# Two plain units instead of four ahead of the paired products, in three of four feed-forward half steps

## The chip, the cores and the metric

The kernel runs on one core of a Trainium2 chip. The metric is the device time of one execution in microseconds (us), as the median of several runs. TensorE (PE) multiplies matrices from SBUF, the on-chip memory, into PSUM, its accumulators of eight banks. VectorE (DVE), ScalarE (ACT) and GpSimd (POOL) do the elementwise work, and SyncE (SP) starts most transfers from the main memory. Each engine works through its own list of instructions in a fixed order, and waits where an input is not there yet.

## What is computed

A two-layer encoder over 512 tokens of width 1024, all in 32-bit floats. Each layer is a feed-forward half step, a token mixer, a cross-attention and another feed-forward half step, so there are four half steps in all. Only they are touched by the change:

```python
def swiglu(h, w_in, w_out):
    a, b = jnp.split(h @ w_in, 2, axis=-1)
    return (jax.nn.silu(a) * b) @ w_out

for l in range(2):
    x = x + 0.5 * swiglu(rms_norm(x, ffn1_norm[l]), ffn1_w_in[l], ffn1_w_out[l])
    ...  # token mixer, cross-attention
    x = x + 0.5 * swiglu(rms_norm(x, ffn2_norm[l]), ffn2_w_in[l], ffn2_w_out[l])
```

The hidden width is 2816, or 22 hidden tiles of 128.

## The kernel before

**Three multiplications for one.** A float matrix product is made of three on fp32r operands (`mm3`, L472 to L475): each operand is split into a rounded high half and a low half that is the rest, and the products high by high, high by low and low by high are added up in PSUM. So every operand, weights too, costs one ScalarE cast (the high half, `whi` for weights, L444) and one VectorE subtraction (the low half, `wlo`, L445); for activations both stand in `split_to` (L602 and L603).

**A half step** has three kinds of work, in the order that `ffn_order` writes out by hand.

- A *plain unit* (`pair_unit`) makes the two halves a and b of one hidden tile: 8 input blocks by 2 columns by 3, so 48 multiplications with 512 columns. `gated` then makes silu(a)·b: VectorE multiplies by the norm's row (L652), ScalarE applies silu (L653), GpSimd multiplies (L654), VectorE multiplies by b (L655), and the result is split (L602, L603).
- A *pair* makes two hidden tiles by Strassen's scheme in Winograd's form. Its seven products (`S1`, `A11`, `A12`, `S2`, `S3`, `A22`, `S4`) have 24 multiplications each, with 256 columns. Each product takes a block of weights that is split when it is due, and a moving operand `mv`, made once per half step by the task `combos`. That task first normalizes the whole input into the buffers `xn` (L674). Four of the moving operands are sums of quarters of the input (`total`, L684, and its split); three are quarters that are written in place over `xh` and `xl` (`in_place`), which the plain units must have finished reading. The weights of S1, S2 and S4 are sums as well: the transfers add two blocks, and VectorE adds A11 (L452) and later A12 (L456) in the same buffer. Each pair also has seven VectorE additions that combine the products (L754), two multiplications (L778) and two splits.
- An *output tile* (`out_tile`) multiplies the hidden tiles of one block with `w_out`, three multiplications of 512 columns for each hidden tile, and VectorE adds the result to x (L728). Eight such tiles belong to each block of hidden tiles.

Before the change every half step has 4 plain units, then 2 output tiles of their block, and then 9 pairs in blocks of 3, 2, 2 and 2, with two or four output tiles within each pair; 8 output tiles end it.

**What sets the order.** The program order is as the source emits it. Weights are split three parts ahead of their use (`LOOK` in `take`), into four buffers, so a split waits for the matrix engine to be done with the part four before it. Tasks such as `combos` advance by one step at each `tick`, after a gated unit or an output tile. A scheduler then lays each engine's list out, and may draw an instruction ahead of one that it expects to wait; that list is what runs.

## Time and profile before

| What | Before |
|---|---|
| Median of three runs | 2607.92 us (2606.85 to 2607.95) |
| The profiled execution, device time | 2608.38 us |
| Its span, first instruction to last | 2606.5 us |
| TensorE busy | 2571.5 us, 99% of the span |
| VectorE busy | 1826.2 us, 70% |
| ScalarE busy | 1321.3 us, 51% |
| GpSimd busy | 337.2 us, 13% |
| Mean granted clock of TensorE | 0.996 of full speed |

The profile's page gives the busy time of each engine and the chain of waits that ended last. The timeline lists instructions with start, duration and the idle time in front of them, in brackets with what ended it. For pipelined engines a duration is longer than the distance to the next start; where instructions follow without a wait, this text goes by that distance. The half steps begin at about 0, 958, 1305 and 2243 us of the span; mixer and cross-attention lie between the first and the second, and between the third and the fourth.

### The profile page before, as it was taken

Reading aid. Unit: us, or ns where it says so; the run is one execution under the profiler, and the core shown is the slowest. Engines: PE = TensorE matmul, PEld = TensorE weight load, DVE = VectorE, ACT = ScalarE, POOL = GpSimd, SP = SyncE. Lnnn points to the kernel's source line nnn. Section 1 sums busy time; section 2 is a strip of 40 time slices with the busy share of each in tenths; the row PEclk is TensorE's granted clock in tenths of the full one; section 3 lists DMA queues with packets and bytes.
Section 4 is the critical chain, followed back from the end, with each engine's and each line's share of the span. In section 5 each row is a group of like instructions: output and inputs, shape, how many; then the busy total and the mean of one; then the engine's idle time right before and its main releaser. Section 6 shows DMA issues by size and latency. Waiting matters only on the chain.

```text
span 2606.5 us, 36643 instructions
## 1 busy us (share of the span) xinstructions
PE 2571.5 (99%) x14784; PEld 2260.2 (87%) x14784; DVE 1826.2 (70%) x2536; ACT 1321.3 (51%) x1861; POOL 337.2 (13%) x294
## 2 busy tenths in 40 slices
PE   8999999999999999999999999999999999999997
PEld 7999978878888888999889999887888888899996
DVE  7867786776655558767788677877675664787675
ACT  5433457876634444434454333579575353444344
POOL 1000035100121021000110000351000300200001
PEclk9999999999999999999999999999999999999999
DMA  6555442222233253645517553321223234345541
GB/s 204 155 153 145 114 137 73 73 82 81 89 112 115 83 176 97 171 137 146 161 65 194 146 146 85 131 95 57 81 81 97 97 130 126 117 135 157 144 124 65
DMA packets 78234, 311.36 MB, mean 119 GB/s; under 512 B 8304, under 2 KB 14064, under 8 KB 69104
## 3 DMA queue, kind: packets, MB, share of 16 engines
q1 hardware_dynamic: 66976, 269.18, 31.0%
q0 software_dynamic: 10368, 37.75, 8.7%
q8 instruction: 115, 1.88, 0.3%
q10 hardware_dynamic: 720, 2.09, 0.2%
q14 instruction: 55, 0.45, 0.1%
HBM read 306.90 MB, written 2.10 MB: 119 GB/s over the span
## 4 chain that ended last, share of the span: by engine, by line
PE 90%; ACT 5%; DVE 3%; DMA 1%; POOL 1%; issue 1%; DVEq 0%; ACTq 0%; SPq 0%; POOLq 0%
PE ps L474 29%; PE ps L473 29%; PE ps L475 29%; PE ps L1132 1%; PE ps L1120 1%; PE ps L1103 1%; ACT whi L444 1%; DVE wlo L445 1%; DVE slot L603 0%; DMA x<-in_xt 0%; DVE xl L537 0%; POOL slot L654 0%; ACT L909 0%; ACT L919 0%; PE ps L1433 0%
## 5 line engine op out<-in xcount | busy, mean ns | idle before, releaser
L473 PE MATMUL ps<-slot,whi 128*128 128x256 f32 (+1 forms) x2436 | 812.9, 335 | 6.9 <-ACT slot L602 6.9
L474 PE MATMUL ps<-slot,whi 128*128 128x256 f32 (+1 forms) x2436 | 814.3, 334 | 0.9 <-DVE slot L603 0.9
L475 PE MATMUL ps<-slot,wlo 128*128 128x256 f32 (+1 forms) x2436 | 810.9, 334 | 0.0
L444 ACT CAST whi<-stage 128x1024 fp32r<-128x1024 f32 (+3 forms) x394 | 346.4, 881 | 509.5 <-PE ps L474 412.9
L473 PE MATMUL ps<-xh,whi 128*128 128x512 f32 (+1 forms) x1760 | 597.6, 340 | 6.6 <-ACT xh L536 3.3
L474 PE MATMUL ps<-xl,whi 128*128 128x512 f32 (+1 forms) x1760 | 594.5, 338 | 0.3 <-DVE xl L537 0.3
L475 PE MATMUL ps<-xh,wlo 128*128 128x512 f32 (+1 forms) x1760 | 594.2, 338 | 0.0
L445 DVE TENSOR_TENSOR wlo<-stage,whi 128x1024 fp32r<-128x1024 f32 (+3 forms) x394 | 415.5, 1056 | 148.0 <-ACT whi L444 145.3
L473 PEld LDWEIGHTS ps<-slot,whi 128*128 128x128 f32 x2436 | 463.1, 190 | 54.0 <-ACT slot L602 10.0
L474 PEld LDWEIGHTS ps<-slot,whi 128*128 128x128 f32 x2436 | 463.7, 190 | 46.0 <-DVE slot L603 2.4
L475 PEld LDWEIGHTS ps<-slot,wlo 128*128 128x128 f32 x2436 | 463.1, 190 | 46.2
L444 ACT CAST whi<-slot 128x1024 fp32r<-128x1024 f32 x252 | 265.3, 1053 | 433.4 <-PE ps L474 318.5
L473 PEld LDWEIGHTS ps<-xh,whi 128*128 128x128 f32 x1760 | 334.3, 190 | 45.9 <-DVE slot L1256 4.9
L474 PEld LDWEIGHTS ps<-xl,whi 128*128 128x128 f32 x1760 | 334.4, 190 | 38.3 <-DVE xl L537 1.6
L475 PEld LDWEIGHTS ps<-xh,wlo 128*128 128x128 f32 x1760 | 334.2, 190 | 35.1
L445 DVE TENSOR_TENSOR wlo<-slot,whi 128x1024 fp32r<-128x1024 f32 x252 | 307.8, 1222 | 66.0 <-ACT whi L444 66.0
L754 DVE TENSOR_TENSOR slot<-ps,slot 128x512 f32<-128x512 f32 x252 | 170.6, 689 | 140.9 <-PE ps L475 139.7
L428 POOL DMA_DIRECT2D slot<-in_wts x72 | 62.9, 874 | 1204.3 <-DMA slot<-in_wts 1053.3
L602 ACT CAST slot<-slot 128x512 fp32r<-128x512 f32 (+2 forms) x165 | 106.0, 649 | 147.3 <-POOL slot L1290 44.6
L728 DVE SCALAR_TENSOR_TENSOR x<-ps,x 128x512 f32<-128x512 f32 (+1 forms) x161 | 110.5, 686 | 88.7 <-PE ps L475 88.6
L603 DVE TENSOR_TENSOR slot<-slot,slot 128x512 fp32r<-128x512 f32 (+2 forms) x165 | 123.0, 754 | 51.7 <-ACT slot L602 51.7
L603 DVE TENSOR_TENSOR slot<-ps,slot 128x512 fp32r<-128x512 f32 (+1 forms) x144 | 92.8, 655 | 38.7 <-ACT slot L602 38.1
(205 smaller groups left out, 2667.7 us busy)
## 6 DMA issues: line engine op xcount, KB each, us to landing
slot<-in_wts SPq DMA_DIRECT2D x180, 512.0 KB, 4.2
stage<-in_wts SPq DMA_DIRECT2D x141, 512.0 KB, 3.6
stage<-in_wts SPq DMA_DIRECT2D x68, 1024.0 KB, 4.8
slot<-in_wts POOLq DMA_DIRECT2D x72, 512.0 KB, 6.1
stage<-in_wts SPq DMA_DIRECT2D x24, 768.0 KB, 6.0
slot<-in_memt SPq DMA_DIRECT2D x6, 512.0 KB, 3.7
slot<-in_bd SPq DMA_DIRECT2D x4, 512.0 KB, 3.6
out<-slot SPq DMA_DIRECT2D x8, 256.0 KB, 2.3
```

The costliest lines, as they stand in the source:

```text
L428: pool.dma_start(out=t, in_=a22 if nm == "S1" else a11, accum_op=ALU.add)
L444: mark["whi"] = act.copy(hi[:, 0:n], t).ins
L445: dve.tensor_tensor(lo[:, 0:n], t, hi[:, 0:n].bitcast(F32), op=ALU.subtract)
L473: pe.matmul(ps, lhsT=ah, rhs=bh, start=start, stop=False)
L474: pe.matmul(ps, lhsT=ah, rhs=bl, start=False, stop=False)
L475: pe.matmul(ps, lhsT=al, rhs=bh, start=False, stop=stop)
L602: act.copy(hi, src)
L603: return dve.tensor_tensor(lo, src, hi.bitcast(F32), op=ALU.subtract).ins
L728: dve.scalar_tensor_tensor(x[:, m, cs], ps, 0.5, x[:, m, cs], op0=ALU.mult, op1=ALU.add)
L754: dve.tensor_tensor(r.f, ps, other.f, op=op)
L1103: pe.matmul(ps, lhsT=qt[e].r[:, c0:c0 + P], rhs=kk.r[:, k0:k0 + 512], start=part == 0, stop=part == 1)
L1120: pe.transpose(ps[:, kt * P:(kt + 1) * P], pexp.f[:, i * 512 + kt * P:i * 512 + (kt + 1) * P], ident)
```

## The change

The first half step keeps its 4 units and its blocks. The other three get 2 units, blocks of 3, 2, 3 and 2 pairs, and all 8 output tiles of the units' block (now of two hidden tiles) ahead of the first pair; the first three pairs then have no output tiles within them, and the later ones have 4, 4, 3, 3, 2, 4 and 4. So two hidden tiles of each of these half steps are made by a pair and no longer by two units. In all four half steps the products on quarters in place, A11 and A12, come ahead of S1, and `combos` makes the two in-place operands before the sums. The weights of a block of two hidden tiles are split for two output tiles at a time (`per_part`).

```diff
-NPLAIN = 4
-PAIR_BLOCKS = (3, 2, 2, 2)
-AHEAD = 2
-PER_PAIR = (2, 2, 2, 4, 4, 4, 4, 4, 4)
-PRODUCTS = ("S1", "A11", "A12", "S2", "S3", "A22", "S4")
-OUT_AT = {2: ("S2", "A22"), 4: ("A11", "S2", "S3", "A22")}
+PRODUCTS = ("A11", "A12", "S1", "S2", "S3", "A22", "S4")
+OUT_AT = {0: (), 2: ("S2", "A22"), 3: ("S2", "S3", "A22"), 4: ("A12", "S2", "S3", "A22")}
...
+class HalfStep:
+    def __init__(self, plain, blocks, ahead, per_pair):
+        self.plain, self.pairs, self.last = plain, sum(blocks), len(blocks)
+        self.at = [0, plain]
+        o = [("unit", j) for j in range(plain)] + [("block", 0)]
+        ready = [("out", 0, m) for m in range(KD)]
+        o += [ready.pop(0) for _ in range(ahead)]
...
+    def per_part(self, b):
+        return 4 // self.size(b) if self.size(b) < 4 else 1
...
+FIRST = HalfStep(4, (3, 2, 2, 2), 2, (2, 2, 2, 4, 4, 4, 4, 4, 4))
+OTHER = HalfStep(2, (3, 2, 3, 2), 8, (0, 0, 0, 4, 4, 3, 3, 2, 4, 4))
+def half_step(l, w_in):
+    return FIRST if l == 0 and w_in == "ffn1_w_in" else OTHER
...
-            elif c0 == "A11":
+            elif c0 == "S1":
                 dve.tensor_tensor(x0, x0, self.buf["A11"], op=ALU.add)
                 self.fetch("A11")
                 self.fetch("S1")
...
+            while not done:
+                yield
+            in_place("A11", 0, 0)
+            ws.fetch("S3")
+            in_place("A12", 1, 0)
+            yield
             t1, c1 = total("S1", b11, b12, ALU.subtract)
-            ws.fetch("S3")
-            yield
             t2, c2 = total("S2", b22, c1, ALU.add)
...
-            while not done:
-                yield
-            in_place("A11", 0, 0)
...
-            in_place("A12", 1, 0)
             total("A22", b21, c2, ALU.subtract)[0].free()
```

How the lists of the engines change is shown at three places. In the rows a number behind a name tells one buffer or bank from another; line numbers of the changed kernel are some 14 to 18 higher.

**VectorE, second half step, behind the last plain unit.** Before, from the first multiplication of the last unit's `gated` on. `slot12`, `slot13` and `slot7` hold weights of the pairs, `slot10` and `slot0` the normalized input, `slot4` a temporary, and `x` is the residual stream:

```order
L652 TENSOR_TENSOR slot4_8409<-ps_8421,srow_8251 128x512
L445 TENSOR_TENSOR wlo_8492<-slot13_8269,whi_8491 128x1024
L655 TENSOR_TENSOR slot4_8409<-slot4_8409,ps_8422 128x512
L603 TENSOR_TENSOR xl_85<-slot0_8272,xh_84 128x4x256 x2
L603 TENSOR_TENSOR slot2_7446<-slot4_8409,slot2_7446 128x512
L684 TENSOR_TENSOR slot4_8409<-slot0_8272,slot4_8409 128x1024
L728 SCALAR_TENSOR_TENSOR x_83<-ps_8499,x_83 128x512
L684 TENSOR_TENSOR slot4_8409<-slot10_396,slot0_8272 128x1024
L603 TENSOR_TENSOR slot6_6894<-slot4_8409,slot6_6894 128x1024
L445 TENSOR_TENSOR wlo_8519<-slot7_8042,whi_8518 128x1024
L603 TENSOR_TENSOR slot5_5151<-slot4_8409,slot5_5151 128x1024
L728 SCALAR_TENSOR_TENSOR x_83<-ps_8522,x_83 128x512
```

After, from the last unit's first multiplication on, up to the first two output tiles' additions (`x`); `slot9` is the unit's gated product, `wlo_8350` belongs to `w_out`:

```order
L667 TENSOR_TENSOR slot9_8257<-ps_8278,srow_8251 128x512
L689 SCALAR_TENSOR_TENSOR slot0_8272<-x_83,par_79,srow_8251 128x512 x2
L670 TENSOR_TENSOR slot9_8257<-slot9_8257,ps_8279 128x512
L459 TENSOR_TENSOR wlo_8350<-stage_8221,whi_8349 128x512
L617 TENSOR_TENSOR xl_85<-slot10_508,xh_84 128x4x256
L617 TENSOR_TENSOR slot1_1865<-slot9_8257,slot1_1865 128x512
L617 TENSOR_TENSOR xl_85<-slot0_8272,xh_84 128x4x256
L745 SCALAR_TENSOR_TENSOR x_83<-ps_8353,x_83 128x512
L745 SCALAR_TENSOR_TENSOR x_83<-ps_8367,x_83 128x512
```

It goes on from the first sum; `slot4` takes the sums, `wlo_8386` and `wlo_8412` are the low halves of the weights of the products A11 and A12:

```order
L699 TENSOR_TENSOR slot4_8375<-slot10_508 128x1024
L459 TENSOR_TENSOR wlo_8386<-slot13_8269,whi_8385 128x1024
L699 TENSOR_TENSOR slot4_8375<-slot0_8272,slot4_8375 128x1024
L617 TENSOR_TENSOR slot2_7446<-slot4_8375,slot2_7446 128x1024
L745 SCALAR_TENSOR_TENSOR x_83<-ps_8389,x_83 128x512
L617 TENSOR_TENSOR slot3_3975<-slot4_8375,slot3_3975 128x1024
L699 TENSOR_TENSOR slot4_8375<-slot10_508,slot0_8272 128x1024
L745 SCALAR_TENSOR_TENSOR x_83<-ps_8400,x_83 128x512
L459 TENSOR_TENSOR wlo_8412<-slot7_8042,whi_8411 128x1024
L617 TENSOR_TENSOR slot6_6894<-slot4_8375,slot6_6894 128x1024
L745 SCALAR_TENSOR_TENSOR x_83<-ps_8415,x_83 128x512
L699 TENSOR_TENSOR slot4_8375<-slot0_8272,slot4_8375 128x1024
```

The list goes on with the rest of the sums, and then the weights of S1 (`wlo_8434`) and S2 (`wlo_8460`):

```order
L617 TENSOR_TENSOR xl_85<-slot0_8272,xh_84 128x4x256
L745 SCALAR_TENSOR_TENSOR x_83<-ps_8425,x_83 128x512
L617 TENSOR_TENSOR slot5_5151<-slot4_8375,slot5_5151 128x1024
L459 TENSOR_TENSOR wlo_8434<-slot12_8268,whi_8433 128x1024
L745 SCALAR_TENSOR_TENSOR x_83<-ps_8441,x_83 128x512
L466 TENSOR_TENSOR slot12_8268<-slot12_8268,slot13_8269 128x1024
L745 SCALAR_TENSOR_TENSOR x_83<-ps_8449,x_83 128x512
L771 TENSOR_TENSOR slot11_8457<-ps_8490,slot11_8457 128x512
L459 TENSOR_TENSOR wlo_8460<-slot12_8268,whi_8459 128x1024
```

Before, S1's sum, A11's quarter and S1's weights stand in front of these rows, under units 2 and 3. After, all four sums stand behind the last unit, and the weights of A12, S1 and S2 behind the sums.

**TensorE, second half step, where the pairs begin.** Before, the end of the second output tile ahead of the pairs (`ps_8522`), one early step each of the first and second tile, and then S1's product (`ps_8543`):

```order
L474 MATMUL ps_8522<-slot2_7446,whi_8423 128x512
L475 MATMUL ps_8522<-slot2_7446,wlo_8424 128x512
L473 MATMUL ps_8499<-slot2_7446,whi_8381 128x512
L473 MATMUL ps_8522<-slot2_7446,whi_8423 128x512
L473 MATMUL ps_8543<-slot1_3975,whi_8453 128x256
L474 MATMUL ps_8543<-slot1_3975,whi_8453 128x256
L475 MATMUL ps_8543<-slot1_3975,wlo_8454 128x256
```

After, the end of product A11 (`ps_8458`), the start of A12 (`ps_8490`) and of S1 (`ps_8523`):

```order
L488 MATMUL ps_8458<-xl_85,whi_8385 128x256
L489 MATMUL ps_8458<-xh_84,wlo_8386 128x256
L487 MATMUL ps_8490<-xh_84,whi_8411 128x256
L488 MATMUL ps_8490<-xl_85,whi_8411 128x256
L487 MATMUL ps_8523<-slot2_7446,whi_8433 128x256
L488 MATMUL ps_8523<-slot2_7446,whi_8433 128x256
L489 MATMUL ps_8490<-xh_84,wlo_8412 128x256
L487 MATMUL ps_8490<-xh_84,whi_8411 128x256
```

The list has two multiplications of S1, on weights `whi_8433`, between the second and the third of A12, which is the first that reads `wlo_8412`; behind the 24th of A12 it goes on with the third of S1, which reads `wlo_8434`.

**VectorE, first half step, up to the last unit's first multiplication by the norm's row.** Before, from behind unit 2's own first multiplication (`ps_329`) to unit 3's (`ps_403`):

```order
L684 TENSOR_TENSOR slot10_396<-slot7_311 128x1024
L445 TENSOR_TENSOR wlo_406<-stage_269,whi_405 128x512
L655 TENSOR_TENSOR slot3_299<-slot3_299,ps_330 128x512
L603 TENSOR_TENSOR slot11_398<-slot10_396,slot11_398 128x1024
L603 TENSOR_TENSOR slot9_389<-slot3_299,slot9_389 128x512
L445 TENSOR_TENSOR wlo_436<-slot4_306,whi_435 128x1024
L603 TENSOR_TENSOR xl_85<-slot7_311,xh_84 128x4x256
L452 TENSOR_TENSOR slot4_306<-slot4_306,slot5_307 128x1024
L652 TENSOR_TENSOR slot10_396<-ps_403,srow_258 128x512
```

After, the same stretch (unit 3 is now `ps_396`):

```order
L459 TENSOR_TENSOR wlo_399<-stage_269,whi_398 128x512
L699 TENSOR_TENSOR slot10_508<-slot7_311 128x1024
L670 TENSOR_TENSOR slot3_299<-slot3_299,ps_330 128x512
L699 TENSOR_TENSOR slot10_508<-slot8_312,slot10_508 128x1024
L617 TENSOR_TENSOR slot9_389<-slot3_299,slot9_389 128x512
L617 TENSOR_TENSOR slot11_510<-slot10_508,slot11_510 128x1024
L617 TENSOR_TENSOR slot12_514<-slot10_508,slot12_514 128x1024
L459 TENSOR_TENSOR wlo_429<-slot5_307,whi_428 128x1024
L617 TENSOR_TENSOR xl_85<-slot7_311,xh_84 128x4x256
L699 TENSOR_TENSOR slot10_508<-slot7_311,slot8_312 128x1024
L667 TENSOR_TENSOR slot3_299<-ps_396,srow_258 128x512
```

Ahead of unit 3's multiplication there are now the sums S2 and S3 and the split of S2, and the addition to the weights of S1 is gone from there.

## Rows read from the trace of the kernel before

**Rows 1.** The page: busy time of each engine, and shares of the last-ending chain.
```profile
PE 2571.5 (99%) x14784; PEld 2260.2 (87%) x14784; DVE 1826.2 (70%) x2536; ACT 1321.3 (51%) x1861; POOL 337.2 (13%) x294
PE 90%; ACT 5%; DVE 3%; DMA 1%; POOL 1%; issue 1%; DVEq 0%; ACTq 0%; SPq 0%; POOLq 0%
```

**Rows 2.** Timeline of TensorE: start, duration, line, operation; pitch of 512 and 256 columns.
```profile
985.57 0.39 PE L473 MATMUL ps<-xh,whi 128*128 128x512 f32 x1
...
996.45 0.39 PE L473 MATMUL ps<-xh,whi 128*128 128x512 f32 x1
...
1011.75 0.28 PE L473 MATMUL ps<-xh,whi 128*128 128x256 f32 x1
...
1014.63 0.28 PE L473 MATMUL ps<-xh,whi 128*128 128x256 f32 x1
```

**Rows 3.** Timeline of TensorE, second half step: start of unit 2, and the last unit's end.
```profile
980.13 0.39 PE L473 MATMUL ps<-xh,whi 128*128 128x512 f32 x1
...
1005.75 0.39 PE L475 MATMUL ps<-slot,wlo 128*128 128x512 f32 x1
1006.81 0.85 PE L473 MATMUL ps<-slot,whi 128*128 128x512 f32 x3 [0.68 <-ACT slot L602]
...
1008.44 0.28 PE L473 MATMUL ps<-slot,whi 128*128 128x256 f32 x1
1009.03 0.50 PE L474 MATMUL ps<-slot,whi 128*128 128x512 f32 x1 [0.31 <-DVE slot L603]
```

**Rows 4.** Busy time by stretch: us, then busy (count) of PE, PEld, DVE, ACT, POOL.
```profile
980.14:1001.89 21.75, 21.75 (x97) 18.01 (x96) 17.04 (x21) 8.19 (x11) 2.74 (x2) 1.00 0.15 49
...
1007.33:1038.00 30.67, 30.36 (x227) 28.92 (x227) 30.64 (x36) 16.02 (x19) 1.76 (x2) 1.00 0.45 123
```

**Rows 5.** Timeline of VectorE, second half step, around the end of unit 1.
```profile
980.27 0.75 DVE L674 SCALAR_TENSOR_TENSOR slot<-x,par,srow 128x512 f32<-128x512 f32 x1
980.93 0.68 DVE L652 TENSOR_TENSOR slot<-ps,srow 128x512 f32<-128x512 f32 x1
...
984.50 0.67 DVE L655 TENSOR_TENSOR slot<-slot,ps 128x512 f32<-128x512 f32 x1
```

**Rows 6.** Timeline of VectorE, second half step, first pair: instructions without a wait between.
```profile
1015.29 0.69 DVE L728 SCALAR_TENSOR_TENSOR x<-ps,x 128x512 f32<-128x512 f32 x1
1015.89 1.22 DVE L684 TENSOR_TENSOR slot<-slot,slot 128x1024 f32<-128x1024 f32 x1
1017.02 1.23 DVE L445 TENSOR_TENSOR wlo<-slot,whi 128x1024 fp32r<-128x1024 f32 x1
```

**Rows 7.** Groups of VectorE's work in one later pair (1056 to 1081.4 us): busy, mean ns.
```profile
L445 DVE TENSOR_TENSOR wlo<-slot,whi 128x1024 fp32r<-128x1024 f32 x7 | 8.6, 1221 | 2.4 <-ACT whi L444 2.4
```

**Rows 8.** Timeline of TensorE, first half step: the wait behind unit 3, and after it.
```profile
59.79 0.39 PE L475 MATMUL ps<-slot,wlo 128*128 128x512 f32 x1
62.71 0.85 PE L473 MATMUL ps<-slot,whi 128*128 128x512 f32 x3 [2.54 <-ACT slot L602]
...
64.02 0.41 PE L473 MATMUL ps<-slot,whi 128*128 128x256 f32 x1
64.24 0.42 PE L474 MATMUL ps<-slot,whi 128*128 128x256 f32 x1
...
67.42 0.28 PE L474 MATMUL ps<-slot,whi 128*128 128x256 f32 x1
67.54 0.28 PE L475 MATMUL ps<-slot,wlo 128*128 128x256 f32 x1
```

**Rows 9.** Timeline of TensorE, third and fourth half step: the same waits behind unit 3.
```profile
1354.35 0.85 PE L473 MATMUL ps<-slot,whi 128*128 128x512 f32 x3 [0.67 <-ACT slot L602]
...
2293.85 0.50 PE L474 MATMUL ps<-slot,whi 128*128 128x512 f32 x1 [0.29 <-DVE slot L603]
```

More of the change, by code (lines that the diff above doesn't have):

```diff
@@ L77, with size @@
 BRANCH_ORDER = branch_order()
-def ffn_order():
-    o = [("unit", j) for j in range(NPLAIN)] + [("block", 0)]
-    ready = [("out", 0, m) for m in range(KD)]
-    o += [ready.pop(0) for _ in range(AHEAD)]
-    i = 0
-    for b, n in enumerate(PAIR_BLOCKS):
-        for _ in range(n):
-            for nm in PRODUCTS:
-                o.append(("product", i, nm))
-                if nm in OUT_AT[PER_PAIR[i]]:
-                    o.append(ready.pop(0))
-            i += 1
-        assert not ready
-        o.append(("block", b + 1))
-        ready = [("out", b + 1, m) for m in range(KD)]
-    return o + ready
-FFN_ORDER = ffn_order()
-BLOCK_AT = [0, NPLAIN]
-for _n in PAIR_BLOCKS:
-    BLOCK_AT.append(BLOCK_AT[-1] + 2 * _n)
+class HalfStep:
[5 more added lines that the diff above has]
+        o += [ready.pop(0) for _ in range(ahead)]
+        i = 0
+        for b, n in enumerate(blocks):
+            self.at.append(self.at[-1] + 2 * n)
+            for _ in range(n):
+                for nm in PRODUCTS:
+                    o.append(("product", i, nm))
+                    if nm in OUT_AT[per_pair[i]]:
+                        o.append(ready.pop(0))
+                i += 1
+            assert not ready
+            o.append(("block", b + 1))
+            ready = [("out", b + 1, m) for m in range(KD)]
+        self.order = o + ready
+    def size(self, b):
+        return self.at[b + 1] - self.at[b]
+    def per_part(self, b):
[4 more added lines that the diff above has]
+    return FIRST if l == 0 and w_in == "ffn1_w_in" else OTHER
 def plan():
@@ L132, in ffn @@
         at = {}
-        for kind, i, *rest in FFN_ORDER:
+        hs = half_step(l, w_in)
+        for kind, i, *rest in hs.order:
             if kind == "unit":
-                first = l == 0 and i == 0 and w_in == "ffn1_w_in"
+                first = hs is FIRST and i == 0
                 add((w_in, l, i), [256, 256, 512, 1024] if first else [1024, 1024],
@@ L419, in fetch @@
             self.next[nm] += 1
-            if n == sum(PAIR_BLOCKS):
+            if n == self.count:
                 return
@@ L669, in combos @@
         def combos():
-            ws.open_pairs()
+            ws.open_pairs(hs.pairs)
             ws.fetch("S1")
@@ L716, in out_tile @@
         def out_tile(b, m):
-            nj = BLOCK_AT[b + 1] - BLOCK_AT[b]
-            last = b == len(PAIR_BLOCKS)
-            hi, lo = ws.take((w_out, l, b, m // 2))
+            nj, e = hs.size(b), hs.per_part(b)
+            last = b == hs.last
+            if m % e == 0:
+                mv["out"] = ws.take((w_out, l, b, m // (2 * e)))
+            hi, lo = (w[:, m % e * nj * P:(m % e + 1) * nj * P] for w in mv["out"])
             tail = last and m == KD - 1 and isinstance(nxt, FinalNorm)
@@ L793, in ffn @@
         run = None
-        for kind, i, *rest in FFN_ORDER:
+        for kind, i, *rest in hs.order:
             if kind == "unit":
@@ L810, in ffn @@
                     done.append(True)
-                elif i == len(PAIR_BLOCKS):
+                elif i == hs.last:
+                    mv.pop("out")
                     for _, _, r in mv.values():
```

21 lines of the change are left out of this document (12 added, 9 removed).

## The prediction

> **What bounds the kernel now.** I read the page first. TensorE is busy 99% of the span and makes up 90% of the chain that ended last [rows 1]; so time can go only where TensorE gets less to do, and comes in wherever it has to wait. Next the timeline of TensorE, for the price of a multiplication: 48 of them with 512 columns take 996.45 − 985.57 = 10.88 us, 0.2267 us each; 24 with 256 columns take 1014.63 − 1011.75 = 2.88 us, 0.12 us each, a little more than half [rows 2]. Then the place that the change touches, behind the last plain unit. Before, TensorE loses little there: 1006.81 instead of 1005.75 + 0.23 is 0.83 us, and 1009.03 instead of 1008.44 + 0.12 is 0.47 us, 1.3 us in all [rows 3]; the third and fourth half step show the same waits [rows 9]. Last, who else is close to its limit there: VectorE is busy for 30.64 of 30.67 us from 1007.33 us on, while TensorE is busy for 30.36 [rows 4]. Both are full at once, and under units 2 and 3 VectorE had 17.04 us of work in 21.75 us to get there without a backlog [rows 4]. That is the reader's picture: TensorE is the bound, but at the start of the pairs VectorE is only just in time.
>
> **What the multiplications give.** In three half steps two units become one pair: 2 × 10.88 = 21.76 us go and 7 × 2.88 = 20.16 us come [rows 2], a gain of 1.6 us each, 4.8 us together. The output tiles have as many multiplications as before, and the waits of 1.3 us go with the place where they stood; what comes for them is the next part.
>
> **What stands behind the last unit now.** It ends 10.88 us after its start, at 980.13 us by the trace, where unit 2 begins now [rows 3]. VectorE's list from that point is fixed, as the rows in the section on the change show it. Up to the low half of S2's weights (`wlo_8460`) it has 13 instructions of 512 columns (two gated multiplications, a split of an output weight, the low half of the gated product, eight output tiles, one combination), two normalizations and 16 instructions of 1024 columns (three quarters in place, four sums, their four low halves, the weights of A11, A12, S1 and S2, and one addition to weights). Without waits between, one of 512 columns takes 1015.89 − 15.29 = 0.60 us, one of 1024 takes 1017.02 − 15.89 = 1.13 us [rows 6], and a normalization takes 980.93 − 980.27 = 0.66 us [rows 5]. That is 7.8 + 1.3 + 18.1 = 27.2 us. To this comes that VectorE gets to the list 0.3 to 0.8 us after the unit's end (0.8 in [rows 5], less if ScalarE's earlier order frees it), and that it waits for GpSimd's multiplication between the two gated ones, 984.50 − 980.93 = 3.57 us from one to the other [rows 5], of which it fills 0.60 + 1.32. Late start and wait come to between 1.3 and 2.5 us; I take 1.8. So S2's low half is ready 28.5 to 29.7 us after the unit's end, by my choice 29.0.
>
> TensorE has, until it needs that half, 48 multiplications of the output tiles (10.88 us), the products A11, A12 and S1 (8.64 us) and two of S2 (0.24 us), 19.76 us [rows 2]. The difference, **9.2 us, is waiting**, and no other work stands on TensorE's list to hide it: there are only two multiplications of S1 between the second and third of A12. The same sum up to the earlier points tells where: up to `wlo_8412` VectorE has 8 × 0.60 + 1.3 + 9 × 1.13 + 1.8 = 18.1 us against 14.2 us, so 3.9 us are lost by then (about 1 us in the output tiles, where the last unit's gated product comes late as it does now, the rest ahead of A12's third multiplication); up to `wlo_8434` it is 24.9 against 16.9 us, another 4 us ahead of S1's third; the last 1 to 1.5 us come ahead of S2's. Before, the same VectorE work met units 2 and 3; now it meets half the TensorE work.
>
> Behind that VectorE has no deficit. A pair without output tiles has 9 instructions of 1024 columns (the seven of [rows 7] and the two additions to weights) and 11 of 512, 10.2 + 6.6 = 16.8 us, against 20.16 us of TensorE. So the three pairs without output tiles cost nothing more, and the backlog isn't paid back either, since TensorE is the bound again. The Trainium skill, "Perfetto Trace Analysis", section "Optimization Strategy", advises to interleave stretches whose most-contended engine differs, which speaks against taking the output tiles out of the first pairs. By it these pairs would become VectorE's; by the count above they stay TensorE's, so it adds nothing to the sum there, and the advice bites only at the transition already counted.
>
> **The clock.** After TensorE's wait of 2.54 us in the first half step, its multiplications of 256 columns start 64.24 − 64.02 = 0.22 us apart, and from 67.42 us on they are back at 0.12 us [rows 8]: the clock was at the lower of its two levels, 1.2 in place of 2.4 GHz, for some 3.4 us, in which 1.6 us of work were lost. After the waits of 0.68 and 0.31 us the 256-column pitch stays at 0.12 us [rows 2, 3]. The waits ahead of A12 and S1 are on either side of 2.54 us. A part of a slow stretch would lie where TensorE waits anyway. I take 1.0 us for each half step, with ends of 0 and 3.3 us (no fall; two falls, none of it hidden).
>
> **The first half step** keeps its units, and only the order changes. Ahead of unit 3's gated product VectorE now has seven instructions of 1024 columns where it had five, 2.3 us more, and this product already holds TensorE up (from 59.79 + 0.23 to 62.71 us) [rows 8]. TensorE's list has seven 256-column multiplications to fill, 0.8 us. I take +1.2 us, with ends of 0 (the sums then are out of the way of what follows) and 3.
>
> **Edits that I cost at nothing.** The split of weights for two output tiles at a time has the same columns as before. From A11's and A12's fetch to their next use there are now five products where there were seven and six, still 14 us; S1's double buffer gets one product more. On SP's and GpSimd's lists the pairs' first transfers stand where they stood, ahead of the units' gated products, and the moved fetch of S3 passes nothing. The early move of A11 and A12 into `xh` and `xl` only needs the last unit done. If such a fetch were late, the first pairs would lose its delay each.
>
> **The sum.** Per changed half step 9.2 + 1.0 − 1.3 − 1.6 = +7.3 us; three of them 21.9, the first 1.2, together +23.1 us on the profiled execution's 2608.4 us, which is 2631.5. The median of the runs shown lies 0.5 us under the profiled one, so I predict **2631 us**. With the low ends (8.7 us of waiting, no fall of the clock, nothing in the first half step) it is 2608 + 3 × 5.8 = 2625, with the high ends (9.9, 3.3 and 3) 2608 + 3 × 10.3 + 3 = 2642.
>
> **The rivals.**
> - *Faster: VectorE's backlog is gone in time.* The place is the same list. It decides at 19.76 + 1.3 + 1.6 = 22.7 us: if S2's low half is ready sooner than that after the last unit, each half step gains. For it speaks that VectorE has (21.75 − 17.04) / 2 = 2.4 us free under a unit, going by units 2 and 3 [rows 4], and that the first half step's list does draw two sums ahead of a unit's end. Against it: the four sums and their low halves, 8 × 1.13 = 9.0 us, stand behind the last unit's gated product on the list, which can't begin before that unit ends. If it held wholly, the time would be 2607.9 − 3 × (1.6 + 1.3) + 1.2 = 2600; with half of the old waits left, 2602. Chance 5%.
> - *No change: half the backlog.* The list is 23 us long in effect, by some overlap that the rows don't show, and the gain is just eaten up: 2608. Chance 4%.
> - *The clock falls after each of the two longer waits.* For it speaks the row behind 2.54 us [rows 8], against it that A12's wait may be shorter than this. Price: 3.3 instead of 1.0 us, 3 × 2.3 = 6.9 us more, 2638. The Trainium skill, "TensorE: Matmul & The Clock Gate", section "HAM oscillation — how this bites in real kernels", tells of a kernel that falls back to the low clock at every tile because it waits at every tile; by that page this rival would be the forecast. Chance 16%.
> - That the change doesn't do what it says can be left out: the lists show the units gone and the products in their new order.
>
> **How the numbers follow.** The forecast has 72% and lies at 2622 to 2636; the clock rival 16%, faster 5%, no change 4%, and 3% for something slower still (a late fetch). The range goes from 2620 to 2643: it holds the forecast and the clock rival with the ends of the unknown costs. About 0.2%, 5 us, is what a measurement of this kernel can tell from no change. Faster by more than that: 5%; within it: 4%; slower: 91%.
>
> **What would show it.** In the changed kernel's trace of the second, third and fourth half step: TensorE idle 2 to 4 us ahead of the third multiplication of A12 and again of S1, and shorter ahead of S2's, each time ended by VectorE's low half of weights; VectorE without idle time over 1 us for some 25 us behind the last unit, apart from the wait for GpSimd; a pair without output tiles at about 20.2 us without waits; slow stretches of the clock at three more places; VectorE's share of the chain up from 3%. Wrong would be: TensorE's first pair without waits (then the list isn't what binds), or waits ended by ScalarE or a transfer, or waits in the later pairs.

## The result, and the profile after

| | Before | After |
|---|---|---|
| Median of four runs of each | 2607.93 us (2606.85 to 2610.25) | 2636.80 us (2634.64 to 2637.28) |
| Ratio | 1 | 1.0104, 95% interval 1.0092 to 1.0117 |
| Profiled execution; its span | 2608.38; 2606.5 us | 2634.64; 2632.9 us |

The change makes the kernel 1.0% slower, 28.9 us. The profiled executions differ by 26.3 us, since that of the changed kernel is the fastest of its four. The page of the changed kernel, the lines that answer to [rows 1]; further down, two groups of multiplications with the idle time before them and what ended it:

```profile
PE 2578.6 (98%) x15000; PEld 2277.0 (86%) x15000; DVE 1850.1 (70%) x2554; ACT 1332.2 (51%) x1861; POOL 335.2 (13%) x294
...
PE 87%; DVE 5%; ACT 5%; DMA 1%; POOL 1%; issue 1%; DVEq 0%; ACTq 0%; SPq 0%; POOLq 0%
...
L489 PE MATMUL ps<-slot,wlo 128*128 128x512 f32 (+1 forms) x2532 | 842.1, 333 | 9.1 <-DVE wlo L459 9.1
...
L489 PE MATMUL ps<-xh,wlo 128*128 128x256 f32 (+1 forms) x1736 | 580.3, 334 | 6.7 <-DVE wlo L459 6.7
```

VectorE's share of the chain rose from 3 to 5%, and 15.8 us of TensorE's idle time end with a low half of weights (`wlo`). The timeline of TensorE shows where, in the second half step and then in the third (start, duration, operation, and the idle time in brackets):

```profile
984.98 0.50 PE L488 MATMUL ps<-slot,whi 128*128 128x512 f32 x1 [0.61 <-DVE slot L617]
...
989.48 0.73 PE L487 MATMUL ps<-slot,whi 128*128 128x512 f32 x2 [0.81 <-ACT slot L616]
...
1002.59 0.38 PE L489 MATMUL ps<-xh,wlo 128*128 128x256 f32 x1 [2.17 <-DVE wlo L459]
...
1009.46 0.58 PE L489 MATMUL ps<-slot,wlo 128*128 128x256 f32 x1 [3.98 <-DVE wlo L459]
...
1356.90 0.39 PE L489 MATMUL ps<-xh,wlo 128*128 128x256 f32 x1 [2.16 <-DVE wlo L459]
...
1363.78 0.39 PE L489 MATMUL ps<-slot,wlo 128*128 128x256 f32 x1 [2.49 <-DVE wlo L459]
```

The first two stand in the output tiles, then come A12's third multiplication and S1's third. Measured from one start to the next, beyond the pitch of [rows 2], the waits of the second half step are 0.77 + 0.97 + 2.33 + 4.15 = 8.2 us; in the third they are 6.7, in the fourth 7.0 us. On VectorE's timeline the instructions that end them stand without a gap between their neighbours:

```profile
988.03 0.69 DVE L670 TENSOR_TENSOR slot<-slot,ps 128x512 f32<-128x512 f32 x1 [1.19 <-POOL slot L669]
...
1000.72 0.68 DVE L745 SCALAR_TENSOR_TENSOR x<-ps,x 128x512 f32<-128x512 f32 x1
1001.32 1.22 DVE L459 TENSOR_TENSOR wlo<-slot,whi 128x1024 fp32r<-128x1024 f32 x1
...
1008.19 1.22 DVE L459 TENSOR_TENSOR wlo<-slot,whi 128x1024 fp32r<-128x1024 f32 x1
...
1012.31 2.36 DVE L459 TENSOR_TENSOR wlo<-slot,whi 128x1024 fp32r<-128x1024 f32 x2
```

VectorE's last idle time there is the one for GpSimd at 988.03 us. The length of a half step can be read from one row sum to the next (TensorE's multiplications by a matrix of ones, with which each norm adds up its squares). Against before it grew by 6.8 us in the second half step, 7.5 in the third and 6.9 in the fourth. The first half step took 3.2 us more, the stretches between and the tail some 2.6 us more, and TensorE's first row sum came 0.7 us earlier: 26.4 us in the span.

### The profile page after: what moved, and what is told of

Read it like the earlier page. It is cut to its first block, busy times and chain, and to the rows that moved or that the text cites. A ratio compares the mean times of both kernels' runs of the same rounds, so it can differ in the third digit from the quotient of the medians.

```text
span 2632.9 us, 37143 instructions
## 1 busy us (share of the span) xinstructions
PE 2578.6 (98%) x15000; PEld 2277.0 (86%) x15000; DVE 1850.1 (70%) x2554; ACT 1332.2 (51%) x1861; POOL 335.2 (13%) x294
## 3 DMA queue, kind: packets, MB, share of 16 engines
q8 instruction: 117, 1.92, 0.3%
## 4 chain that ended last, share of the span: by engine, by line
PE 87%; DVE 5%; ACT 5%; DMA 1%; POOL 1%; issue 1%; DVEq 0%; ACTq 0%; SPq 0%; POOLq 0%
PE ps L487 28%; PE ps L489 28%; PE ps L488 28%; PE ps L1150 1%; PE ps L1138 1%; DVE slot L617 1%; PE ps L1121 1%; DVE wlo L459 1%; ACT whi L458 1%; DVE x L745 1%; DVE slot L699 1%; DVE slot L689 1%; DVE xl L617 0%; ACT L927 0%; DMA x<-in_xt 0%
## 5 line engine op out<-in xcount | busy, mean ns | idle before, releaser
L487 PE MATMUL ps<-slot,whi 128*128 128x512 f32 (+1 forms) x2532 | 842.0, 334 | 10.8 <-ACT slot L616 10.8
L489 PE MATMUL ps<-slot,wlo 128*128 128x512 f32 (+1 forms) x2532 | 842.1, 333 | 9.1 <-DVE wlo L459 9.1
L488 PE MATMUL ps<-slot,whi 128*128 128x512 f32 (+1 forms) x2532 | 843.5, 333 | 1.8 <-DVE slot L617 1.8
L487 PE MATMUL ps<-xh,whi 128*128 128x256 f32 (+1 forms) x1736 | 582.7, 336 | 5.7 <-DVE slot L1274 3.3
L489 PE MATMUL ps<-xh,wlo 128*128 128x256 f32 (+1 forms) x1736 | 580.3, 334 | 6.7 <-DVE wlo L459 6.7
L488 PE MATMUL ps<-xl,whi 128*128 128x256 f32 (+1 forms) x1736 | 580.2, 334 | 0.3 <-DVE xl L551 0.3
L487 PEld LDWEIGHTS ps<-slot,whi 128*128 128x128 f32 x2532 | 483.9, 191 | 58.6 <-ACT slot L616 13.6
L489 PEld LDWEIGHTS ps<-slot,wlo 128*128 128x128 f32 x2532 | 484.1, 191 | 55.5 <-DVE wlo L459 9.8
L488 PEld LDWEIGHTS ps<-slot,whi 128*128 128x128 f32 x2532 | 484.8, 191 | 48.4 <-DVE slot L617 4.5
L459 DVE TENSOR_TENSOR wlo<-stage,whi 128x1024 fp32r<-128x1024 f32 (+3 forms) x370 | 397.9, 1078 | 180.7 <-ACT whi L458 166.6
L458 ACT CAST whi<-slot 128x1024 fp32r<-128x1024 f32 x273 | 285.3, 1049 | 426.0 <-PE ps L488 338.1
L459 DVE TENSOR_TENSOR wlo<-slot,whi 128x1024 fp32r<-128x1024 f32 x273 | 332.7, 1220 | 50.1 <-ACT whi L458 49.7
```

Source lines behind the costliest of these rows:

```text
L458: mark["whi"] = act.copy(hi[:, 0:n], t).ins
L459: dve.tensor_tensor(lo[:, 0:n], t, hi[:, 0:n].bitcast(F32), op=ALU.subtract)
L487: pe.matmul(ps, lhsT=ah, rhs=bh, start=start, stop=False)
L488: pe.matmul(ps, lhsT=ah, rhs=bl, start=False, stop=False)
L489: pe.matmul(ps, lhsT=al, rhs=bh, start=False, stop=stop)
```

## The experiments

Each ratio is to runs of the kernel before that were taken beside it.

| Kernel | Median, us | Ratio to before, 95% interval |
|---|---|---|
| new order alone, 4 units | 2612.66 | 1.0014 (1.0004 to 1.0024) |
| 2 units, old order | 2630.39 | 1.0082 (1.0066 to 1.0098) |
| changed, first half step in old order | 2632.70 | 1.0087 (1.0072 to 1.0102) |
| changed, no low halves of the sums | 2618.35 | 1.0034 (1.0020 to 1.0047) |
| changed, no casts of the sums | 2634.95 | 1.0099 (1.0084 to 1.0114) |
| changed, two low halves twice | 2639.07 | 1.0111 (1.0096 to 1.0126) |
| changed, two output tiles ahead | 2636.62 | 1.0105 (1.0088 to 1.0121) |
| changed, sums on GpSimd | 2644.03 | 1.0133 (1.0117 to 1.0149) |
| the same, `gated` without GpSimd | 2642.14 | 1.0128 (1.0112 to 1.0144) |
| changed, `gated` without GpSimd | 2629.25 | 1.0071 (1.0056 to 1.0086) |
| before, `gated` without GpSimd | 2604.61 | 0.9985 (0.9976 to 0.9995) |
| the same, norms' additions on VectorE | 2601.00 | 0.9963 (0.9950 to 0.9976) |

The theory is that VectorE's list behind the last unit is longer than the TensorE work beside it. The rivals are that the order of products makes the loss, or ScalarE's casts, or the missing output tiles in the pairs.

**Which part of the change costs.** The new order alone, with four units everywhere:

```diff
 def half_step(l, w_in):
-    return FIRST if l == 0 and w_in == "ffn1_w_in" else OTHER
+    return FIRST
...  # the smaller parts of the very first unit stay with that unit
```

> All four half steps have 4 plain units and 2 output tiles ahead again, as before; only the new order of the products and of the combos task stays. Backlog theory (VectorE's list behind the last unit is too long for the TensorE work that stands beside it): units 2 and 3 are there again to cover the sums, the waits of the second to fourth half step fall to 0 to 2 us each, the first half step keeps its wait of about 5 us ahead of its output tiles: 2610 to 2616 us. Rival (the order alone costs, because the weights of A11, A12 and S1 come due in a row that the buffers don't allow): most of the loss stays, 2625 to 2637 us.

It measured +3.7 us by the ratio. In its trace the other three half steps each lie within 0.2 us of before, and nearly all of the difference stands ahead of the second: some 2.2 us in the first half step itself, the rest ahead of it and behind it. TensorE's timeline, first and second half step, shows a longer wait in the first and the waits of [rows 3] again in the second:

```profile
66.16 0.80 PE L487 MATMUL ps<-slot,whi 128*128 128x512 f32 x1 [4.19 <-ACT slot L616]
...
1011.61 0.73 PE L487 MATMUL ps<-slot,whi 128*128 128x512 f32 x2 [0.67 <-ACT slot L616]
...
1013.83 0.50 PE L488 MATMUL ps<-slot,whi 128*128 128x512 f32 x1 [0.29 <-DVE slot L617]
```

The units alone, with the old order:

```diff
+OLD = ("S1", "A11", "A12", "S2", "S3", "A22", "S4")
...
-FIRST = HalfStep(4, (3, 2, 2, 2), 2, (2, 2, 2, 4, 4, 4, 4, 4, 4))
-OTHER = HalfStep(2, (3, 2, 3, 2), 8, (0, 0, 0, 4, 4, 3, 3, 2, 4, 4))
+FIRST = HalfStep(4, (3, 2, 2, 2), 2, (2, 2, 2, 4, 4, 4, 4, 4, 4), OLD)
+OTHER = HalfStep(2, (3, 2, 3, 2), 8, (0, 0, 0, 4, 4, 3, 3, 2, 4, 4), OLD)
...  # combos and the fetches: with OLD, sums S1, S2, S3 ahead of the quarters again
```

> Two units, the new blocks and the eight output tiles ahead of the pairs in the last three half steps, but the old order of products (S1, A11, A12, S2, ...) and of the combos task everywhere. The first half step is then the one of before. Backlog theory: the same VectorE work stands behind the last unit, only sorted differently; counted as in the prediction, A12's low half is ready 26.1 us after the unit's end where TensorE needs it after 16.9, so about 9 us of waits in each of three half steps as in the prediction, or about what the changed kernel showed, 7 to 8: 2608 + 3 x (5 to 7.5), so 2624 to 2632 us. Rival (the new order of products makes the loss, and two units alone would gain 1.6 us a half step): 2603 to 2608 us.

The second to fourth half step took 7.0, 5.9 and 6.4 us more than before, with the new order 6.8, 7.5 and 6.9. The waits only stand at other products, now in A11 and A12, and behind them in a later one:

```profile
999.77 0.38 PE L492 MATMUL ps<-xl,whi 128*128 128x256 f32 x1 [2.29 <-DVE xl L621]
...
1002.03 0.58 PE L493 MATMUL ps<-xh,wlo 128*128 128x256 f32 x1 [1.89 <-DVE wlo L463]
...
1008.71 0.39 PE L491 MATMUL ps<-slot,whi 128*128 128x256 f32 x1 [0.92 <-ACT whi L462]
```

So in these half steps the units make the loss: the order of products changes it by 0.2, 1.6 and 0.5 us.

The first half step in the old order, the rest as changed:

```diff
-FIRST = HalfStep(4, (3, 2, 2, 2), 2, (2, 2, 2, 4, 4, 4, 4, 4, 4))
+FIRST = HalfStep(4, (3, 2, 2, 2), 2, (2, 2, 2, 4, 4, 4, 4, 4, 4), OLD)
...  # OTHER keeps the new order
```

> The first half step gets the old order of products and of the combos task back, the other three stay as changed. If the first half step's extra is its own (two more sums ahead of unit 3's gated product, and a second slow stretch of the clock): its wait goes back from 5.1 to 2.7 us, and the time is 3 to 4 us below the changed kernel's, 2632 to 2634 us. If the shift seen there was something else (clock, start): no difference that can be measured.

Its median is 4 us below the changed kernel's, as expected, though the two intervals overlap. But its trace shows a wait of 4.79 us, not 2.7, and a first half step only 0.4 us shorter than the changed kernel's. The reason stands further ahead: ScalarE's cast of weights that a transfer has just brought, before, after and in this kernel (ScalarE's timeline), and then this kernel's wait on TensorE:

```profile
33.81 2.00 ACT L444 CAST whi<-stage 128x1024 fp32r<-128x1024 f32 x2 [1.92 <-DMA stage<-in_wts]
```
```profile
33.14 2.00 ACT L458 CAST whi<-stage 128x1024 fp32r<-128x1024 f32 x2 [1.79 <-DMA stage<-in_wts]
```
```profile
35.46 2.01 ACT L462 CAST whi<-stage 128x1024 fp32r<-128x1024 f32 x2 [4.34 <-DMA stage<-in_wts]
```
```profile
64.34 1.22 PE L491 MATMUL ps<-slot,whi 128*128 128x512 f32 x2 [4.79 <-ACT slot L620]
```

From this cast to the end of the wait it is 62.71 − 33.81 = 28.9 us before [rows 8], 28.9 here, and 28.9 in the kernel with two units and the old order; after it is 65.43 − 33.14 = 32.3 us. With the new order alone it is 32.8 us, and 32.3 again in three of the kernels below. So the order costs 3.4 us on that path. When the transfer lands moves the wait on top of it: the cast starts between 32.2 and 37.6 us in the profiled executions.

**Is it VectorE's list?** Four VectorE instructions less, then four ScalarE casts less, then two VectorE instructions more:

```diff
-                split_to(o.r[:, 0:1024], o.r[:, 1024:2048], r.f)
+                act.copy(o.r[:, 0:1024], r.f)
...  # the high half serves as the low half
```

> The changed kernel without the low halves of the four sums (VectorE has four subtractions of 1024 columns less in each half step, about 4.5 us; the products read the high half in their place, so a part of the computation is left out). ScalarE and TensorE have the same work. Backlog theory: in each of the last three half steps the waits of 7 to 8 us shrink by 4 to 5, to 2 to 4 us, and the slow stretches of the clock get fewer; the first half step's wait shrinks by about 1 us: 2636.8 - 3 x (4 to 5.5) - 1 to 2, so 2618 to 2624 us. Rival (ScalarE's casts or the four weight buffers bind, and VectorE is only the last in their chain): under 1 us a half step, 2633 to 2637 us.

The last three half steps took 2.4, 1.8 and 1.9 us more than before, so 4.4, 5.7 and 5.0 us less than in the changed kernel, for 4 × 1.13 = 4.5 us of VectorE work. Of the two long waits one is left (TensorE, second half step):

```profile
1001.54 0.39 PE L489 MATMUL ps<-slot,wlo 128*128 128x256 f32 x1 [1.71 <-DVE wlo L459]
```

```diff
-                split_to(o.r[:, 0:1024], o.r[:, 1024:2048], r.f)
+                dve.tensor_tensor(o.r[:, 1024:2048], r.f, r.f, op=ALU.add)
...  # this serves as both halves
```

> The changed kernel without ScalarE's four casts of the sums in each half step (four of 1024 columns, some 4 us of ScalarE); VectorE keeps its four instructions of 1024 columns there, now without the wait for a cast, and the products read its result for both halves, so a part of the computation is left out. Backlog theory: ScalarE was not the bound, VectorE's list is as long as before: 2633 to 2638 us. Rival (ScalarE's casts bind): the waits shrink by 3 to 4 us in each of three half steps, 2624 to 2629 us.

The time can't be told from the changed kernel's, and the last three half steps took 6.8, 7.5 and 6.4 us more than before. So ScalarE's casts of the sums don't bind.

```diff
                 split_to(o.r[:, 0:1024], o.r[:, 1024:2048], r.f)
+                if nm in ("S1", "S2"):
+                    dve.tensor_tensor(o.r[:, 1024:2048], r.f, o.r[:, 0:1024].bitcast(F32), op=ALU.subtract)
```

> The changed kernel with the low halves of the sums S1 and S2 computed twice by VectorE: 2 x 1.13 = 2.3 us more VectorE work in each half step, behind the last unit and ahead of S2's weights. Backlog theory: every us on this list is a us of waiting, so 2 to 2.5 us more in each of the last three half steps; in the first both stand ahead of unit 3's gated product, 2.3 us more there too: 2636.8 + 4 x 2.3 = 2646, 2642 to 2649 us. Rival (VectorE has slack, and something else sets the waits): under 3 us more.

Its median is 2.3 us above the changed kernel's, its profiled span 5.6 us, both less than the 9 expected; by the intervals alone the two kernels can't be told apart, so the trace has to show it. In the last three half steps the waits are 9.7, 9.0 and 9.0 us, 1.5 to 2.3 us more than after for 2.3 us of work (A12's is now the longest, S1's is shorter); the half steps themselves took 1.9, 1.0 and 1.8 us more, since the third and fourth have one slow stretch of the clock in place of two. TensorE, second half step:

```profile
1007.95 0.58 PE L489 MATMUL ps<-xh,wlo 128*128 128x256 f32 x1 [5.57 <-DVE wlo L459]
...
1013.69 0.39 PE L489 MATMUL ps<-slot,wlo 128*128 128x256 f32 x1 [1.52 <-DVE wlo L459]
```

In the first half step nothing was added: from the weights' cast to the end of the wait it is 32.3 us as after, since the scheduler put the repeated instruction where the third sum had stood. So the list is the cause, and ScalarE's casts of the sums aren't; but an instruction put on it does not always land ahead of the wait.

**What the eight tiles ahead are worth.**

```diff
-        return 4 // self.size(b) if self.size(b) < 4 else 1
+        return 1
...
-OTHER = HalfStep(2, (3, 2, 3, 2), 8, (0, 0, 0, 4, 4, 3, 3, 2, 4, 4))
+OTHER = HalfStep(2, (3, 2, 3, 2), 2, (2, 2, 2, 4, 4, 3, 3, 2, 4, 4))
```

> The changed kernel with 2 of the units' 8 output tiles ahead of the pairs and 2 within each of the first three pairs, as before the change; the units stay at two, the order of products is the new one, and the output weights are split for one tile at a time. This asks what the eight tiles ahead are worth, and whether pairs without tiles cost anything. Backlog theory: six tiles fewer stand beside the list (8.2 us of TensorE), and six additions fewer on it (3.6 us), so 4.6 us more waiting in each of three half steps, 2646 to 2653 us. Rival (pairs without output tiles starve on VectorE, so tiles within them help): 2630 to 2637 us.

The time is that of the changed kernel and lies within the rival's 2630 to 2637 us; the loss of 10 us or more that the theory expected is missing. The half steps took 6.7, 6.2 and 8.3 us more than before. VectorE's timeline shows a part of the reason: the low halves of A11's and A12's weights start at 983.41 and 989.34 us, 1.2 us before the last unit's end (984.6) and 4.7 us behind it. After, they started at 994.45 and 1001.32 us, 10 and 17 us behind it. The weights of a part are split three parts ahead of their use, so tiles ahead of the pairs push the pairs' weights back on the list. Six tiles fewer take 8.2 us from the TensorE work beside the list, and give back six additions (3.6 us) and weights split sooner; that these make up for all of it is not shown. The long waits now stand at the moving operands (TensorE):

```profile
990.03 0.58 PE L487 MATMUL ps<-xh,whi 128*128 128x256 f32 x1 [3.21 <-ACT xh L616]
...
999.80 0.38 PE L487 MATMUL ps<-slot,whi 128*128 128x256 f32 x1 [0.77 <-ACT slot L616]
...
1001.90 0.38 PE L487 MATMUL ps<-slot,whi 128*128 128x256 f32 x1 [1.71 <-ACT slot L616]
```

The rival's reason, that pairs without tiles starve, isn't borne out: tiles within the pairs bring no gain over the changed kernel. The three pairs without tiles ran as predicted: of the changed kernel's 20.20 us from 1046.00 on (a row of stretches: us, then busy and count of PE, PEld, DVE, ACT, POOL, then clock and transfers), TensorE has 20.20 and VectorE 16.89.

```profile
1046.00:1066.20 20.20, 20.20 (x171) 20.20 (x170) 16.89 (x21) 10.29 (x13) 1.73 (x2) 1.00 0.71 179
```

**Can GpSimd take the sums?**

```diff
-                dve.tensor_tensor(c, a, b, op=op)
+                pool.tensor_tensor(c, a, b, op=op)
```

> The changed kernel with the four sums of each half step computed on GpSimd in place of VectorE; all else stays. VectorE loses four instructions of 1024 columns (4.5 us) from the same list. GpSimd is idle for some 30 us there; its multiplication of 512 columns takes 1.73 us, so four sums take about 14 us. Backlog theory: the waits shrink by 3 to 4.5 us in each of the last three half steps, 2614 to 2625 us. Rival (GpSimd's sums come too late for S1 and S2, or slow VectorE down while both run): no gain or a loss, 2632 to 2645 us.

It is slower still, by 7.2 us in the medians and 10.9 in the profiled executions. Most of that, 8.2 us, stands in the first half step; the other three took 1.4, 0.5 and 1.3 us more than in the changed kernel, where 3 to 4.5 less was expected. GpSimd's timeline and then VectorE's, second half step:

```profile
989.07 2.76 POOL L699 TENSOR_TENSOR slot<-slot 128x1024 f32<-128x1024 f32 x1 [1.36 <-DVE slot L689]
...
997.29 2.39 POOL L699 TENSOR_TENSOR slot<-slot,slot 128x1024 f32<-128x1024 f32 x1
1003.78 2.38 POOL L699 TENSOR_TENSOR slot<-slot,slot 128x1024 f32<-128x1024 f32 x1 [4.10 <-DVE slot L617]
```
```profile
990.11 2.28 DVE L459 TENSOR_TENSOR wlo<-stage,whi 128x512 fp32r<-128x512 f32 x1
...
997.96 3.94 DVE L617 TENSOR_TENSOR xl<-slot,xh 128x1024 fp32r<-128x1024 f32 x2
...
1003.56 1.28 DVE L745 SCALAR_TENSOR_TENSOR x<-ps,x 128x512 f32<-128x512 f32 x2
1004.76 2.49 DVE L617 TENSOR_TENSOR slot<-slot,slot 128x1024 fp32r<-128x1024 f32 x1
```

The first sum ends at 991.83 us, and a VectorE instruction of 0.69 us that began under it ends at 992.39; another sum ends at 1006.16, and one of 1.22 us that began at 1004.76 ends at 1007.25. Each stood still until GpSimd was done. The two additions from 1003.56 on, which read an operand from PSUM, took their usual time under the same sum. The Trainium skill says so: "SBUF — State Buffer", section "SBUF: two separate sides", has the two engines share a pair of ports under an exclusive lock, which a VectorE operation with two SBUF inputs needs too; the trace agrees. Under these three sums VectorE lost 2.28 − 0.69 = 1.6, 3.94 − 2.35 = 1.6 and 2.49 − 1.22 = 1.3 us, and 1.8 us under the fourth (3.03 us at 1010.64 in place of 1.22): 6.3 us for the 4.5 us that it was spared. In the first half step, too, VectorE's instructions are stretched under the sums (one of 1024 columns took 3.39 us); how the 8.2 us come about there was not followed further.

The same holds for GpSimd's multiplication in `gated`, which led to three more kernels:

```diff
-            pool.tensor_tensor(t.f, t.f, row[0], op=ALU.mult)
+            dve.tensor_tensor(t.f, t.f, row[0], op=ALU.mult)
```

With the sums on GpSimd:

> The previous kernel, and besides GpSimd's multiplication within gated goes to VectorE (0.6 us more for each unit there, in place of a wait of 1.2 us for GpSimd's 1.73 us). Backlog theory: the list gets shorter by some 0.6 us for each unit under it and the last unit's gated product is ready about 1 us sooner, so 1 to 2 us less for each half step: 2608 to 2620 us. Rival (VectorE gets 0.6 us more for each unit and nothing in return): equal to the previous kernel or 1 to 3 us above it.

The theory's 2608 to 2620 us is missed by far: the second to fourth half step stayed at 7 to 9 us more than before, as in the previous kernel, and only the first gained, 4.7 us. The median can't be told from the previous kernel's, as the rival had it.

The changed kernel with this edit alone:

> The changed kernel with GpSimd's multiplication within gated moved to VectorE. From the run with the sums on GpSimd: a VectorE instruction with both inputs in SBUF stands still until GpSimd's has ended (2.28 us in place of 0.69), so GpSimd's 1.73 us cost VectorE about as much as they take, and VectorE does the same work in 0.60 us. In the changed kernel this multiplication stretches five normalizations (4.42 us instead of 3.4) and makes VectorE wait 1.2 us for the last unit. Theory: the list behind the last unit gets about 1 us shorter, the waits of 0.8 and 1.0 us in the output tiles get shorter too, so 1 to 2 us less in each of the last three half steps and 2 to 3 us in the first: 2627 to 2632 us. Rival (the list only gets 0.6 us longer): 2636 to 2639 us.

The short waits in the output tiles of the last three half steps are gone (0.77 + 0.97 us after), those for A12's and S1's weights stay (A12's grew to 3.25 us in each), and the median is 7.5 us lower. The first half step's 3.2 us are gone too: from the weights' cast to the end of the wait it is 27.6 us. In the kernel before with this edit, which comes next, it is 27.6 us as well (only its cast starts 3.1 us sooner). So the new order lengthens that path only while GpSimd is in it.

The kernel before with this edit alone, and then with the norms' additions on VectorE as well:

> The kernel before with GpSimd's multiplication within gated moved to VectorE, and nothing else. If the waits behind the last unit (1.3 us in each of three half steps, 2.7 us in the first) hang on the way through GpSimd, they shrink by about 1 us each: 2602 to 2606 us. If VectorE's list binds there, 0.6 us more for each of the units makes up for it: 2607 to 2612 us.

```diff
-        def __init__(self, gain, adder=pool):
+        def __init__(self, gain, adder=dve):
```

> The kernel before with GpSimd's multiplication within gated and also the additions of squares of the norms (55 of 512 columns, 1.57 us each on GpSimd) moved to VectorE. If GpSimd's instruction holds VectorE up in general, and the chain at the end of a half step runs through these additions, another 1 to 4 us below the kernel with the first move alone: 2600 to 2604 us. If VectorE has no room at the end of the half steps (55 x 0.6 = 33 us more): 2605 to 2612 us.

Both are faster than the kernel before, the second by 0.37%. Its page has the point in one line:

```profile
PE 2569.5 (99%) x14784; PEld 2260.1 (87%) x14784; DVE 1828.0 (70%) x2607; ACT 1322.9 (51%) x1861; POOL 225.3 (9%) x223
```

VectorE does 71 instructions of 512 columns more than in [rows 1], 71 × 0.60 = 43 us, and is busy for only 1.8 us more: before, it had spent the rest standing still under the 112 us of work that GpSimd no longer has. The traces bear this out one by one. In the kernel before, 82 VectorE instructions took over 1.3 times the median of their kind (the same operation and shape, with or without an input from PSUM), 64.6 us too much in all, and each of them ran beside a GpSimd instruction; in this kernel there are 35, with 24.9 us. The kernel before has such a place within [rows 5], where VectorE seemed to wait for GpSimd (VectorE, two normalizations in 2.44 us in place of 1.4):

```profile
982.13 2.44 DVE L674 SCALAR_TENSOR_TENSOR slot<-x,par,srow 128x512 f32<-128x512 f32 x2
```

## Why the prediction was right, and where it missed

The forecast was 2631 us, the median is 2636.8, within the range of 2620 to 2643 us. It lies just outside the 2622 to 2636 us of the forecast itself and is nearer to the 2638 us of the clock rival, so it is the trace that tells which mechanism held, not the number. Of the 5.8 us between, some 2 stand in the first half step, some 2 in stretches that the change doesn't touch, and the rest is mostly the spread of the runs. Point by point:

- *VectorE's list against TensorE's work*: right. S2's low half was ready at 1012.31 + 1.22 = 1013.5 us, 29.5 us after the last unit's end at 984.0, for 29.0 forecast; TensorE's 19.8 us of work, 8.2 of waits and 1.5 of slow clock make 29.5 as well. The waits stand where they were put, A12's third and S1's third multiplication, 2.3 and 4.2 us for about 3 and 4, and 1.7 us in the output tiles for about 1. The late start and the wait for GpSimd came to 0.85 + 1.26 = 2.1 us, for the 1.8 that was chosen. S2's 1 to 1.5 us didn't come: a slow stretch of the clock behind S1's wait (1009.3 to 1012.4 us) kept TensorE busy until the weights were there.
- *Waits and clock add up*: mis-sized in its parts, right in the sum. Forecast were 9.2 + 1.0 us; measured were 8.2 and one slow stretch of 1.5 us in the second half step, 6.7 and two of them in the third. Where a slow stretch came ahead of S1's wait, the wait was shorter. In the second half step, less 1.3 and 1.6 us, that is 6.8 us, for 7.3, and by 6.8 it grew. The prediction had said that a slow stretch may lie where TensorE waits anyway, but it added the two up as if they were apart; that less waiting and more slow clock nearly cancel is partly luck.
- *The rival of two clock falls*: its mechanism came in the third and fourth half step, where the clock was low behind both long waits, but not its price, since S1's wait shrank from 4.15 to 2.6 and 2.9 us. The rows of stretches of after, behind A12's and S1's wait in the third half step (the last three numbers are the granted clock and the transfers' share and GB/s):

```profile
1356.80:1360.30 3.50, 3.40 (x17) 3.40 (x18) 3.50 (x5) 0.55 (x1) 0.00 (x0) 0.56 0.00 0
...
1363.60:1367.10 3.50, 3.32 (x16) 3.33 (x17) 3.50 (x6) 1.56 (x2) 0.00 (x0) 0.56 0.16 29
```

  Some 16 multiplications in 3.4 us instead of 28. The Trainium skill's section "HAM oscillation — how this bites in real kernels" of "TensorE: Matmul & The Clock Gate" tells of a kernel that waits 3 to 5 us at each tile and is brought back to the low clock each time. Of the seven long waits at these places, one in the first half step and two in each other, two are that long (4.97 and 3.98 us), and there the trace agrees. But the low clock followed four shorter ones as well, of 2.16 to 2.62 us, and not the seventh: behind A12's wait of 2.17 us in the second half step the granted clock stayed at 1.00.
- *The first half step*: mis-sized, and the list misread. Forecast were +1.2 us, measured +3.2 in the trace. The medians of the two kernels that isolate it say about 4, each with an interval of several us. Two VectorE instructions more were counted ahead of unit 3's product, less 0.8 us of TensorE work; there are three (3.4 us). The third, the low half of A12's quarter, stands between unit 3's two multiplications (at 61.66 us; before, behind the second at 61.92), and the list was read only up to the first. VectorE's timeline before and after, and then TensorE's wait after, to be held against the 2.54 us of [rows 8]:

```profile
58.34 0.68 DVE L652 TENSOR_TENSOR slot<-ps,srow 128x512 f32<-128x512 f32 x1
58.94 1.22 DVE L445 TENSOR_TENSOR wlo<-slot,whi 128x1024 fp32r<-128x1024 f32 x1
61.32 0.69 DVE L655 TENSOR_TENSOR slot<-slot,ps 128x512 f32<-128x512 f32 x1 [1.17 <-POOL slot L654]
61.92 2.35 DVE L603 TENSOR_TENSOR xl<-slot,xh 128x1024 fp32r<-128x1024 f32 x2
```
```profile
59.93 0.68 DVE L667 TENSOR_TENSOR slot<-ps,srow 128x512 f32<-128x512 f32 x1
60.53 1.21 DVE L459 TENSOR_TENSOR wlo<-slot,whi 128x1024 fp32r<-128x1024 f32 x1
61.66 1.22 DVE L617 TENSOR_TENSOR xl<-slot,xh 128x1024 fp32r<-128x1024 f32 x1
64.03 0.69 DVE L670 TENSOR_TENSOR slot<-slot,ps 128x512 f32<-128x512 f32 x1 [1.16 <-POOL slot L669]
```
```profile
65.43 0.80 PE L487 MATMUL ps<-slot,whi 128*128 128x512 f32 x1 [4.97 <-ACT slot L616]
```

  Behind the longer wait the clock was low for longer, too: from 65.43 to some 70.2 us, where before it was low from 64.0 to 67.4 us. That cost some 0.7 us more, which the prediction didn't have.
- *Pairs without tiles at no cost, the edits costed at nothing*: as forecast, by 20.20 us of TensorE and 16.89 of VectorE. Behind S2's product TensorE has no wait up to the end of the pairs in the second and the fourth half step. In the third, one of 1.92 us stands ahead of the closing output tiles, where it was 1.14 before. The saving of 1.6 us a half step wasn't measured by itself; the sum of the second half step leaves room for it and for little else.
- *The rest*: the remaining 2 us of the profiled difference stand in stretches that the change doesn't touch. There the clock fell where before it was full: in the first cross-attention (below), and at the last row sums, where the granted clock was 0.61 from 2617.1 to 2621 us.

## What to carry to other kernels

When work of the bounding engine is cut, write down the list of the second engine from that place to the next product that needs it, and compare sums: 29 us against 20 told the result to half a us for a half step. Read such a list up to the instruction that the wait names, not to one ahead of it. Before an engine's list is called full, look for instructions on it that take twice their time: here they stood still under GpSimd, and giving GpSimd's multiplication in `gated` to the "busier" engine made both kernels, before and after, faster.

## What the chip showed that was not expected

A VectorE instruction with two inputs in SBUF didn't run side by side with GpSimd's: 0.69 us became 2.28 us. And the clock falls in places that the change doesn't touch: after, it was low from 527.8 to 531.1 us in the first cross-attention, where before it was full (a row of after, and one of before):

```profile
527.80:531.10 3.30, 3.30 (x9) 2.51 (x9) 3.30 (x7) 3.27 (x5) 0.00 (x0) 0.50 0.24 61
```
```profile
525.00:528.30 3.30, 3.30 (x16) 2.74 (x15) 3.30 (x7) 3.27 (x5) 0.00 (x0) 1.00 0.31 79
```

The same fall shows in five of the twelve kernels of the experiments, with either order in the first half step (the new order alone; the kernel before with one edit in `gated`), and not in the others. What sets it off was not tried.
